# A hybrid GLA and MLA decoder layer: two token tiles run backwards, so that one 128-column matmul serves two tiles at each GLA level

## The chip, the cores and the metric

The kernel runs on one core of a Trainium2 chip. The metric is the device time of one launch in microseconds, of which three runs of the kernel before are shown. A profile of a further execution gives the trace. PE is the matrix engine, PEld its weight loads, DVE the vector engine, ACT the scalar engine, POOL the GpSimd engine, and SP issues most DMAs.

## The reference

One decoder layer on x of 512 tokens by 1024 columns, all in float32. A layer norm is followed by one projection w_in that yields q, k, v, r and a gate of rank 16 for gated linear attention (GLA, four heads, 128 key and 256 value columns each), latents for multi-head latent attention (MLA, eight heads) and two sets of branch gates. Then come the two attentions, their output projections, the gated merge, an output projection, a layer norm, and a squared-ReLU MLP of width 4096 with another layer norm. The part that the change touches is the GLA:

```python
log_a = jax.nn.log_sigmoid((a_lr @ w_gla_a2 + b_gla_a2).astype(jnp.float32)) / GLA_TAU
...
b = jnp.cumsum(gi, axis=2)
diff = b[:, :, :, None, :] - b[:, :, None, :, :]
decay = jnp.exp(jnp.where(causal[:, :, None], diff, -jnp.inf))
scores = jnp.einsum('bhid,bhjd,bhijd->bhij', qi, ki, decay)
o = jnp.einsum('bhij,bhjv->bhiv', scores, vi) + jnp.einsum('bhid,bhdv->bhiv', qi * jnp.exp(b), state)
state = jnp.exp(b_last)[:, :, 0, :, None] * state + jnp.einsum('bhjd,bhjv->bhdv', ki * jnp.exp(b_last - b), vi)
```

Taken over all chunks, the score of query i and key j (j not after i) is the sum over the key columns of q·k times the exponential of the log decays between j and i.

## The kernel before, in words

The 512 tokens are four tiles of 128 (`NT = 4`). Most products are made of float32 values split into two parts: `hi`, a rounded copy, and `lo`, the remainder (`split`, lines 106 to 115, and `pump`, lines 191 and 192, for weights). A product of two split operands is three matmuls: hi·hi, hi·lo and lo·hi (lines 247 to 249 with the activations moving and 281 to 283 with the weights moving). Weights come as a stream of entries: SP loads a raw tile `wraw` ahead of use, ACT rounds it to `whi` (L191), DVE forms the remainder `wlo` (L192), and PE uses both. Every engine works through its own instructions in the order in which the program was written, so an instruction that waits holds up all that stand behind it on that engine.

The program is written by Python generators. `spawn` puts one among the active ones, and each step of a large product calls `tick`, which advances the active ones by one `yield`. So the side work (norms, gates, GLA levels, attention) is laced between the matmuls of the large products, and the places of the `yield`s set the order.

The pieces that matter here:

- `prep` (L504 to L535) turns positions into the sine and cosine tables, and casts the level mask from the loaded int32 `lmi` to `lmask` (bytes) on DVE.
- `latents` (L594 to L630) makes the GLA log decays: the part `at` (L605) and the rounded `aT` (L606) on DVE, four matmuls into `z` (L611), `g` (L615) on DVE, the exponential and logarithm on ACT, and the final subtraction on POOL (L629).
- `r_prep` and `r_acc` (L695) load the weights of the r projection in combinations: SP loads one quarter (L700), and POOL then issues DMAs that add another onto it in place. There are eight such accumulating DMAs at the start, all in POOL's own software queue.
- `h_early` (L1091 to L1097) forms sums and differences of the normalised activations on DVE for the fast product of r.
- `gla_levels(h)` does the scores of one head by halving. At level s (1, 2, 4, ... 256) each block of 2s tokens has a left half of keys and a right half of queries, and the decay from a key to a query splits at the middle into two factors, neither of which exceeds one. `rp[:, 0]` holds the log decay from a token to the end of its block, `rp[:, 1]` that from the beginning of the block. `vec` takes the two exponentials on ACT (L800), multiplies them with k and q on DVE into `M` (L802, one instruction of 512 columns), and `advance` doubles the block on POOL (L794 and L795).
- For levels 2 to 64, line 856 multiplies, tile by tile, the columns of `M` up to the last key (128, 96 or 64 of them) with the 64 query columns of the tile: four matmuls a level. Level 128 (L860) is two matmuls of 128 by 128 and level 256 (L864) two of 128 by 256. These products are in plain float32, and each shows up as two matmul records. `take` copies the wanted entries of the result into `SD` under the mask `lmask` (L812).
- `proj_v` and `silu` evict v and r by head, 256 columns at a time (L112 from `proj_v`, L687).
- `gla_out` multiplies the scores with v, tile by tile.

```python
for tt in range(NT):
    c = slice(tt * P, (tt + 1) * P)
    mm(p[:rows(s), tt * 64:(tt + 1) * 64].rearrange("p (n s) -> p n s", s=s),
       M[:, tt * P:tt * P + rows(s)], pairs(M[:, c], s)[:, :, 1, :], start=True, stop=True)
```

Of the kernel before, what the change touches and what calls it, by code (L numbers as in the profile page):

```python
# [10 lines left out]
F32 = mybir.dt.float32  # L11
# [41 lines left out]
def tile_hybrid_block(ctx: ExitStack, tc: tile.TileContext, I, out, dbg=None):  # L53
# [41 lines left out]

    act = nc.scalar.activation
# [32 lines left out]
    ident = ca[:, 0:P]  # L129
    g_in = ca[:, P:P + NK]  # L130
# [3 lines left out]
    identr = consts.tile([P, P], F32R, name="identr")  # L134
    masks = consts.tile([P, T], F32, name="masks")
# [312 lines left out]
    def ln_transpose(rows, g, b, outs, hf, alt=False, n="h0"):  # L448
        tk = slice(hf * 256, (hf + 1) * 256)
        for k in range(NK):  # L450
# [3 lines left out]
            for i in range(2):  # L454
                nc.tensor.transpose(p[:, i * P:(i + 1) * P], rows[2 * hf + i][:, k * P:(k + 1) * P], ident)
# [27 lines left out]
    act(identr, ident, AF.Copy)  # L483
    cb = consts.tile([P, PACK_B - P], F32, name="cb")
    n0 = PACK_B - P - 32
    for dst, c0, n in ((cb[:, :n0], 0, n0), (masks[:, T - P:], n0, P), (cb[:, n0:], n0 + P, 32)):
        nc.scalar.dma_start(dst, I["c_pack_b"][:, c0:c0 + n])
# [9 lines left out]
    nc.gpsimd.memset(masks[:, :T - P], 0.0)  # L497
# [3 lines left out]
    cs2 = consts.tile([P, NT, ROPE], F32, name="cs2")  # L501
    sn2 = consts.tile([P, NT, ROPE], F32, name="sn2")

    def prep():  # L504
        with tc.issue_after(last_in.ins):
            vts(hbg, bgt, 0.5, None, op0=ALU.mult)
            nc.vector.tensor_copy(lmask, lmi)
        posf = consts.tile([P, NT], F32, name="posf")
        with tc.issue_after(last_in.ins):
            nc.vector.tensor_copy(posf, posi)  # L510
        ang = B([P, NT, 32], F32, "ang")
# [17 lines left out]
        act(sn2[:, :, 32:], angs[0], AF.Sin)  # L529
        act(cs2[:, :, :32], angs[1], AF.Sin)  # L530
        nc.vector.tensor_copy(cs2[:, :, 32:], cs2[:, :, :32])
        vts(sn2[:, :, :32], sn2[:, :, 32:], -1.0, None, op0=ALU.mult)
        yield

    def rope(src, cs, sn, dst, tmp, tmp2):  # L535
        vtt(tmp, src, cs, op=ALU.mult)
        vtt(tmp2[..., 0:32], src[..., 32:64], sn[..., 0:32], op=ALU.mult)
        vtt(tmp2[..., 32:64], src[..., 0:32], sn[..., 32:64], op=ALU.mult)
        gtt(dst, tmp, tmp2, op=ALU.add)
# [92 lines left out]
    def latents2():  # L632
# [5 lines left out]
        for tt in range(NT):  # L638
            src = lat[tt][:, LKR:LKR + ROPE]
            vtt(kt1[:, tt], src, cs2[:, tt], op=ALU.mult)  # L640
            vtt(kt2[:, tt, 0:32], src[:, 32:64], sn2[:, tt, 0:32], op=ALU.mult)
            vtt(kt2[:, tt, 32:64], src[:, 0:32], sn2[:, tt, 32:64], op=ALU.mult)
        vtt(kr, kt1, kt2, op=ALU.add)
# [15 lines left out]
    def lr(t2, s):  # L659
        v = t2[:, 0, :]  # L660
        return bass.AP(tensor=v.tensor, offset=v.offset, ap=[v.ap[0], [2 * s, T // (2 * s)], [T + s, 2], [1, s]])

    def pairs(v, s):
        return v.rearrange("p (n two s) -> p n two s", two=2, s=s)

    Vh = [None] * GH
    Rg = [None] * GH
    ogT = [None] * NK

    def proj_v(hp, guard=None):  # L670
        hs = (2 * hp, 2 * hp + 1)

        def e(a, j, ps):
            for i, h in enumerate(hs):
                if Vh[h] is None:
                    Vh[h] = (A([P, NT, HV], F32R, "vh"), A([P, NT, HV], F32R, "vl"))
                split(ps[:, i * HV:(i + 1) * HV], Vh[h][0][:, a, :], Vh[h][1][:, a, :])
        gemm_tm([PL["v", hp]], hT, T, e, guard=guard, fine=3)

    def silu(j, a, ps):  # L680
        th = B([P, T], F32, "th")
        act(th, ps, AF.Tanh, scale=0.5)
        for i in range(2):
            h = 2 * j + i
            if Rg[h] is None:
                Rg[h] = A([P, NT, HV], F32, "rg")
            stt(Rg[h][:, a, :], th[:, i * HV:(i + 1) * HV], 1.0, ps[:, i * HV:(i + 1) * HV],  # L687
                op0=ALU.add, op1=ALU.mult)
            rgn[h] += 1
# [88 lines left out]
    def rows(s):  # L778
        return P - s if s >= 32 else P

    def gla_levels(h):
# [8 lines left out]

        def advance(s):
            Rv, Pv = pairs(rp[:, 0, :], s), pairs(rp[:, 1, :], s)
            n = T // (2 * s)
            gtt(Rv[:, :, 0, :], Rv[:, :, 0, :], Pv[:, :, 1, s - 1:s].to_broadcast([P, n, s]), op=ALU.add)  # L794
            gtt(Pv[:, :, 1, :], Pv[:, :, 1, :], Pv[:, :, 0, s - 1:s].to_broadcast([P, n, s]), op=ALU.add)  # L795

        def vec(s):
            E = B([P, T], F32, "E")
            for w in range(2):
                act(pairs(E, s)[:, :, w, :], pairs(rp[:, w, :], s)[:, :, w, :], AF.Exp, scale=1.0 / 16.0)  # L800
            M = B([P, T], F32, "M")
            vtt(pairs(M, s), pairs(E, s), lr(qk, s), op=ALU.mult)  # L802
# [4 lines left out]
        def take(s, p):  # L807
            nonlocal s128, s256
            if s <= 64:
                n, m = 64 // s, rows(s)  # L810
                mk = lmask[:m, LEVELS.index(s), :].rearrange("p (n s) -> p n s", s=s)
                nc.vector.copy_predicated(  # L812
                    SDf[:m].rearrange("p (t n two s) -> p t n two s", t=NT, two=2, s=s)[:, :, :, 1, :],
                    mk[:, None].to_broadcast([m, NT, n, s]),
                    p[:m, :256].rearrange("p (t n s) -> p t n s", t=NT, s=s))
# [9 lines left out]
        act(q1, pairs(rp[:, 1, :], 1)[:, :, 1, :], AF.Exp, scale=1.0 / 16.0)  # L825
        xs = [B([P, 2, 192], F32, "x1") for _ in range(2)]
        for i in range(2):
# [3 lines left out]
                qk[:, 1, t2].rearrange("p (t n two) -> p t n two", t=2, two=2)[:, :, :, 1], op=ALU.mult)  # L831
# [12 lines left out]
        for i, p in enumerate(px1):  # L844
# [3 lines left out]
            nc.vector.copy_predicated(d.rearrange("p t (n two) -> p t n two", two=2)[:, :, :, 1],  # L848
                                      lmask[:, 0, None, :].to_broadcast([P, 2, 64]), pt[:, :, P:])
        prev = None  # L850
        while s < T:
            p = PX()
            if s <= 64:
                for tt in range(NT):
                    c = slice(tt * P, (tt + 1) * P)
                    mm(p[:rows(s), tt * 64:(tt + 1) * 64].rearrange("p (n s) -> p n s", s=s),  # L856
                       M[:, tt * P:tt * P + rows(s)], pairs(M[:, c], s)[:, :, 1, :], start=True, stop=True)
            elif s == 128:
                for i in range(2):
                    mm(p[:, i * P:(i + 1) * P], M[:, 2 * i * P:(2 * i + 1) * P],  # L860
                       M[:, (2 * i + 1) * P:(2 * i + 2) * P], start=True, stop=True)
# [17 lines left out]
    def gla_out(h):  # L879
        while SS[h] is None or Vh[h] is None or rgn[h] < NT:  # L880
            yield
# [9 lines left out]
        vh, vl = Vh[h]  # L891
        ss = S([P, NT], F32, "gss")
        ps = []
        for i in range(NT):
# [3 lines left out]
            for j in range(i + 1):  # L898
                mm(o, blk(j, i, 0), vh[:, j, :], start=j == 0, stop=False)
                mm(o, blk(j, i, 0), vl[:, j, :], start=False, stop=False)  # L900
                mm(o, blk(j, i, 1), vh[:, j, :], start=False, stop=j == i)
# [10 lines left out]
        for i in range(NT):  # L912
            o = ps[i // 2][:, (i % 2) * HV:(i % 2 + 1) * HV]
            stt(og[i // 2][:, i % 2, :], o, rs[:, i:i + 1], Rg[h][:, i, :], op0=ALU.mult, op1=ALU.mult)
        yield
        for kk in range(2):
            k = 2 * h + kk
            p = PX()
            for tt in range(NT):
                nc.tensor.transpose(p[:, tt * P:(tt + 1) * P], og[tt // 2][:, tt % 2, kk * P:(kk + 1) * P], ident)  # L920
# [13 lines left out]
    def tables():  # L934
        tab = A([P, 2, T], F32, "tab")
        for i, (src, c0) in enumerate(((cs2, 0), (sn2, 32))):
# [749 lines left out]
```

## Time and profile before

| quantity | value |
|---|---|
| runs (us) | 878.78, 880.04, 885.48; median 880.04 |
| profiled execution | 882.47 us, of which the span is 880.7 |
| granted TensorE clock | 0.997 |
| busy: PE, PEld | 861.2 us, 752.9 us |
| busy: DVE, ACT, POOL | 643.2, 470.2, 198.3 us |
| DMA | 134.60 MB in 95504 packets, 153 GB/s on average |
| level matmuls (L856) | 192 records, from 104.7 to 209.7 us |

The span runs from the first to the last instruction of the profiled execution; the time of that execution is slightly longer than its span. A row of a timeline reads: start, length, engine, line, operation, output <- input, shapes, count, and in brackets the idle time before it with what ended it. Consecutive instructions overlap on an engine, so the starts tell more than the lengths.

### The profile page before, as it was taken

What the parts mean: (1) busy time and instruction counts of PE and PEld (TensorE: products, weight loads), DVE (VectorE), ACT (ScalarE), POOL (GpSimd) and SP (SyncE); (2) the same over time, 40 slices, a digit from 0 to 9 for tenths busy, and PEclk for the clock granted to TensorE, in tenths of its full rate; (3) what the DMA queues carried; (4) which work ended last, traced back from release to release, by engine and by line L of the source; (5) the groups of instructions that cost most, each with busy time, mean ns of one, the idle gap of its engine ahead of it and who ended that gap; (6) DMA issues with size and microseconds to landing.
All of it is one profiled execution on the core that took longest, in us unless ns stands there. A gap on an engine that the chain in (4) does not pass through costs nothing.

```text
span 880.7 us, 13019 instructions
## 1 busy us (share of the span) xinstructions
PE 861.2 (98%) x4804; PEld 752.9 (85%) x4804; DVE 643.2 (73%) x1054; ACT 470.2 (53%) x835; POOL 198.3 (23%) x226
## 2 busy tenths in 40 slices
PE   6999999999999999999999999999999999999996
PEld 5988888889999978888888889988888888888985
DVE  7859969978665646767866878986567546778865
ACT  5556766556465624435655324575366446656820
POOL 1224637854101030300000022005301520141000
PEclk9999999999999999999999999999999999999998
DMA  7995936796638454322136446008922990497312
GB/s 249 277 229 151 328 107 160 227 225 198 163 104 199 130 142 102 102 66 79 49 120 243 140 144 216 1 1 251 259 64 51 299 222 3 104 251 198 120 62 81
DMA packets 95504, 134.60 MB, mean 153 GB/s; under 512 B 12960, under 2 KB 58400, under 8 KB 95440
## 3 DMA queue, kind: packets, MB, share of 16 engines
q1 hardware_dynamic: 73840, 92.36, 33.0%
q0 software_dynamic: 19392, 37.76, 20.0%
q10 hardware_dynamic: 2208, 3.66, 1.2%
q8 instruction: 38, 0.62, 0.3%
q14 instruction: 26, 0.21, 0.1%
HBM read 110.15 MB, written 8.91 MB: 135 GB/s over the span
## 4 chain that ended last, share of the span: by engine, by line
PE 92%; DVE 3%; DMA 2%; ACT 1%; issue 0%; POOLq 0%; SPq 0%; DVEq 0%; POOL 0%; ACTq 0%
PE mm L247 11%; PE mm L248 11%; PE mm L249 11%; PE mm L283 5%; PE mm L281 5%; PE mm L282 5%; PE mm L1210 4%; PE mm L1209 4%; PE mm L1208 4%; PE px L856 2%; PE px L1495 2%; PE px L1494 2%; PE px L1496 2%; DMA res<-ev 2%; PE mm L755 2%; PE mm L754 2%
## 5 line engine op out<-in xcount | busy, mean ns | idle before, releaser
L192 DVE TENSOR_TENSOR wlo<-wraw,whi 128x1024 fp32r<-128x1024 f32 (+1 forms) x102 | 102.0, 1009 | 82.3 <-ACT whi L191 79.2
L191 ACT ACTIVATE whi<-wraw 128x1024 fp32r<-128x1024 f32 (+1 forms) x102 | 86.5, 860 | 86.0 <-PE mm L248 46.6
L248 PE MATMUL mm<-h,whi 128*128 128x512 f32 x224 | 87.2, 389 | 0.0
L247 PE MATMUL mm<-h,whi 128*128 128x512 f32 x224 | 87.1, 390 | 0.0
L249 PE MATMUL mm<-h,wlo 128*128 128x512 f32 x224 | 83.2, 390 | 0.0
L1513 POOL DMA_DIRECT2D res<-ev x42 | 37.4, 1027 | 182.5 <-ACT ev L1511 152.6
L192 DVE TENSOR_TENSOR wlo<-wq,whi 128x1024 fp32r<-128x1024 f32 x44 | 54.5, 1238 | 28.0 <-ACT whi L191 27.9
L191 ACT ACTIVATE whi<-wq 128x1024 fp32r<-128x1024 f32 x44 | 46.5, 1056 | 28.4 <-PE mm L1209 20.0
L1210 PE MATMUL mm<-sh,wlo 128*128 128x256 f32 x176 | 49.9, 283 | 0.0
L1209 PE MATMUL mm<-sh,whi 128*128 128x256 f32 x176 | 49.8, 283 | 0.0
L1208 PE MATMUL mm<-sh,whi 128*128 128x256 f32 x176 | 49.8, 283 | 0.0
L249 PEld LDWEIGHTS mm<-h,wlo 128*128 128x128 f32 x224 | 42.0, 188 | 9.1 <-DVE wlo L192 0.4
L247 PEld LDWEIGHTS mm<-h,whi 128*128 128x128 f32 x224 | 42.1, 188 | 8.7
L248 PEld LDWEIGHTS mm<-h,whi 128*128 128x128 f32 x224 | 42.1, 188 | 8.7
L191 ACT ACTIVATE xh<-wraw 128x1024 fp32r<-128x1024 f32 (+1 forms) x28 | 27.2, 985 | 28.6 <-PE mm L283 16.7
L439 POOL TENSOR_TENSOR mv<-mv,mhalf 128x1 f32<-128x1 f32 x4 | 4.7, 1179 | 157.9 <-DVE mv L438 157.9
L800 ACT ACTIVATE E<-rp 128x256 f32<-128x256 f32 x64 | 26.2, 420 | 24.4 <-POOL rp L795 15.9
L192 DVE TENSOR_TENSOR xl<-wraw,xh 128x1024 fp32r<-128x1024 f32 (+1 forms) x28 | 31.3, 1128 | 8.5 <-ACT xh L191 8.5
L1559 ACT ACTIVATE relu<-mm 128x512 f32<-128x512 f32 x24 | 14.1, 596 | 42.0 <-PE mm L249 42.0
L794 POOL TENSOR_TENSOR rp<-rp 128x256 f32<-128x256 f32 x32 | 30.9, 965 | 22.3 <-ACT E L800 13.5
L971 POOL DMA_DIRECT2D QS<-q x32 | 16.0, 508 | 85.2 <-DMA wraw<-in_w_o_gla_dram 48.5
L795 POOL TENSOR_TENSOR rp<-rp 128x256 f32<-128x256 f32 x32 | 33.4, 1043 | 6.1 <-ACT q L825 2.7
(478 smaller groups left out, 2812.7 us busy)
## 6 DMA issues: line engine op xcount, KB each, us to landing
wraw<-in_w_ff_dram SPq DMA_DIRECT2D x36, 512.0 KB, 5.3
wraw<-in_w_in_dram SPq DMA_DIRECT2D x30, 512.0 KB, 5.1
wq<-in_w_ff_dram POOLq DMA_DIRECT2D x26, 512.0 KB, 9.3
res<-ev POOLq DMA_DIRECT2D x42, 256.0 KB, 9.1
wq<-in_w_in_dram SPq DMA_DIRECT2D x20, 512.0 KB, 6.7
wq<-in_w_in_dram POOLq DMA_DIRECT2D x18, 512.0 KB, 9.8
hsd<-hs SPq DMA_DIRECT2D x16, 256.0 KB, 4.8
xr<-hsd SPq DMA_DIRECT2D x16, 256.0 KB, 3.6
```

The source lines that it names most:

```text
L191: st["ins"] = act(hi[:, k, :n], raw[:, k, :n], AF.Copy)
L192: st["lo"] = vtt(lo[:, k, :n], raw[:, k, :n], f(hi[:, k, :n]), op=ALU.subtract)
L247: mm(o, hi[:, c], xh, start=first, stop=False)
L248: mm(o, hi[:, c], xl, start=False, stop=False)
L249: mm(o, lo[:, c], xh, start=False, stop=last)
L281: mm(o, xh, hi[:, :n], start=opens, stop=False, skip_group_check=share)
L282: mm(o, xh, lo[:, :n], start=False, stop=False, skip_group_check=share)
L283: mm(o, xl, hi[:, :n], start=False, stop=last, skip_group_check=share)
L1208: mm(oa, hi[:, k, c], xh, start=opens and k == 0 and a == 0, stop=False, skip_group_check=True)
L1209: mm(oa, hi[:, k, c], xl, start=False, stop=False, skip_group_check=True)
L1210: mm(oa, lo[:, k, c], xh, start=False, stop=k == 3, skip_group_check=True)
L1513: nc.gpsimd.dma_start(res[tt + t][:, j * T:(j + 1) * T], e, accum_op=ALU.add)
```

## The change

- The tokens of tiles 2 and 3 are stored in reverse order within their tile. That is done where the normalised input is transposed: the transposing matmul takes the identity with its columns reversed (`identJ`). What depends on token order follows: the positions of these tiles are turned by two small transposes, the causal mask of MLA gets a transposed version for them, the outputs are turned back by `identJ` in the transposes of `og` and of the attention weights, and the branch gates are written backwards.
- With that, in tiles 2 and 3 the queries of a block stand left and the keys right. At each level, `M` is laid out in two halves: 256 columns of keys and 256 of queries. The 64 keys of tile t and the 64 of tile t + 2 fill 128 columns, interleaved by blocks, as do their queries, so one matmul of 128 by 128 serves two tiles; two matmuls a level take the place of four. The columns of queries stand in two runs of 64.
- `M` is written by two DVE instructions of 256 columns instead of one of 512, each after its own exponential.
- The level mask now has 512 columns in the new order. The half for tiles 0 and 1 comes from the old load, the half for tiles 2 and 3 from seven further DMAs that POOL issues into a second, zeroed `lmi`, each shifted by s rows. Fourteen DVE casts take the place of one.
- The tables of sine and cosine are kept once, at 32 columns; `kr` is made by a subtraction and an addition.
- v and r of heads 2 and 3 are evicted by 512 columns at once into tiles that the two heads share.

In the order of instructions, the matmul engine has 48 level matmuls where there were 96 for levels 2 to 64, and three transposes more. DVE has 1095 instructions where there were 1056, ACT 791 for 796, POOL 240 for 231. On POOL the mask loads stand behind the fifth accumulating `wq` load and ahead of the sixth. On DVE, seven of the casts stand early (after the input's norms) and seven in the neighbourhood of `aT`: `at`, the first new cast, `aT`, the other six, and then the split of the next weight tile. SP issues 241 instructions as before; a few loads of `wraw` and `wq` change places by one.

```diff
+    def rev(ap):
+        dims = [list(d) for d in ap.ap]
+        step, n = dims[-1]
+        return bass.AP(tensor=ap.tensor, offset=ap.offset + step * (n - 1), ap=dims[:-1] + [[-step, n]])
+
+    def view(ap, off, *dims):
+        return bass.AP(tensor=ap.tensor, offset=ap.offset + off, ap=[list(ap.ap[0])] + [list(d) for d in dims if d[1] > 1])
...
+    identJ = rev(ident)
...
-                nc.tensor.transpose(p[:, i * P:(i + 1) * P], rows[2 * hf + i][:, k * P:(k + 1) * P], ident)
+                nc.tensor.transpose(p[:, i * P:(i + 1) * P], rows[2 * hf + i][:, k * P:(k + 1) * P],
+                                    identJ if hf and n == "h0" else ident)
...
-    act(identr, ident, AF.Copy)
...
-    lmask = consts.tile([P, len(LEVELS), 64], U8, name="lmask")
-    lmi = B([P, len(LEVELS), 64], I32, "lmi")
-    nc.scalar.dma_start(lmi, I["c_lmask"])
+    lmask = consts.tile([P, 512], U8, name="lmask")
+    lmi = [B([P, len(LEVELS), 64], I32, "lmi")]
+    nc.scalar.dma_start(lmi[0], I["c_lmask"])
+
+    def lm_load():
+        lmi.append(B([P, len(LEVELS), 64], I32, "lmi"))
+        nc.gpsimd.memset(lmi[1], 0)
+        for li, s in enumerate(LEVELS):
+            nc.gpsimd.dma_start(lmi[1][s:, li], I["c_lmask"][:P - s, li])
...
-            nc.vector.tensor_copy(lmask, lmi)
...
+        p = PX()
+        nc.tensor.transpose(p[:2, :P], posf[:, 2:], identJ)
+        nc.tensor.transpose(p[:, P:2 * P], masks[:, P:2 * P], ident)
...
+        nc.tensor.transpose(p[:, :2], pr, ident[:2, :2])
...
+        lm_load()
+        yield
+        act(sn, angs[0], AF.Sin)
+        act(cs, angs[1], AF.Sin)
+        yield
+        for s in LEVELS:
+            for d in range(2):
+                src = lmi[d][:, LEVELS.index(s), ::s]
+                nc.vector.tensor_copy(lm(s)[:, d], src[:, None].to_broadcast([P, 2, 64 // s]))
+        yield
...
+            if hp == 1:
+                if a % 2 == 0:
+                    t = [A([P, 2, T], F32R, n) for n in ("vh", "vl")]
+                    for h in hs:
+                        Vh[h] += [[x[:, i, h % 2 * HV:(h % 2 + 1) * HV] for x in t] for i in range(2)]
+                    Vt[hp] = t
+                split(ps, Vt[hp][0][:, a % 2], Vt[hp][1][:, a % 2])
+                return
...
+            stt(Vt["r", j, a // 2][:, a % 2], th, 1.0, ps, op0=ALU.add, op1=ALU.mult)
...
         def vec(s):
             E = B([P, T], F32, "E")
-            for w in range(2):
-                act(pairs(E, s)[:, :, w, :], pairs(rp[:, w, :], s)[:, :, w, :], AF.Exp, scale=1.0 / 16.0)
             M = B([P, T], F32, "M")
-            vtt(pairs(M, s), pairs(E, s), lr(qk, s), op=ALU.mult)
+            for w, src in enumerate((R, G)):
...
+                act(e, halves(src, s, w), AF.Exp, scale=1.0 / 16.0)
+                vtt(m, e, halves(qk[:, w, :], s, w), op=ALU.mult)
...
-                nc.vector.copy_predicated(
-                    SDf[:m].rearrange("p (t n two s) -> p t n two s", t=NT, two=2, s=s)[:, :, :, 1, :],
-                    mk[:, None].to_broadcast([m, NT, n, s]),
-                    p[:m, :256].rearrange("p (t n s) -> p t n s", t=NT, s=s))
+                n = P // s
+                mk = lm(s).rearrange("p d t n -> p d (t n)")
+                nc.vector.copy_predicated(halves(SDf, s, 1), mk[:, :, :, None].to_broadcast([P, 2, n, s]),
+                                          p[:, :256].rearrange("p (d n i) -> p d n i", d=2, i=s))
...
             if s <= 64:
-                for tt in range(NT):
-                    c = slice(tt * P, (tt + 1) * P)
-                    mm(p[:rows(s), tt * 64:(tt + 1) * 64].rearrange("p (n s) -> p n s", s=s),
-                       M[:, tt * P:tt * P + rows(s)], pairs(M[:, c], s)[:, :, 1, :], start=True, stop=True)
+                for t in range(2):
+                    mm(view(p, 64 * t, (P, 2), (1, 64)), M[:, t * P:(t + 1) * P],
+                       view(M, 256 + 64 * t, (P, 2), (1, 64)), start=True, stop=True)
...
-        act(gt[m][:, br, tk], ps, AF.Tanh, scale=0.5, bias=hbg[:, br * NK + m:br * NK + m + 1])
+        g = gt[m][:, br, tk]
+        if tk.start:
+            g, ps = rev(g.rearrange("p (t i) -> p t i", t=2)), ps.rearrange("p (t i) -> p t i", t=2)
+        act(g, ps, AF.Tanh, scale=0.5, bias=hbg[:, br * NK + m:br * NK + m + 1])
```

More of the change, by code (lines that the diff above doesn't have):

```diff
@@ L656, in latents2, with halves, last @@
         KKs.append(KK)
[L659 to L667, printed above, removed]
+    def halves(v, s, right, off=0):
+        if s >= P:
+            return view(v, off + s * right, (256, T // (2 * s)), (1, s))
+        return view(v, off + s * right, (256 - s if right else 256 + s, 2), (2 * s, P // s), (1, s))
+    def last(v, s, right):
+        if s >= P:
+            return view(v, 2 * s - 1 if right else s - 1, (129, T // (2 * s))).to_broadcast([P, T // (2 * s), s])
+        o = view(v, 2 * s - 1 if right else s - 1, (257 - 2 * s if right else 257, 2), (2 * s, P // s))
+        return o[:, :, :, None].to_broadcast([P, 2, P // s, s])
+    Vh = [[] for _ in range(GH)]
+    Rg = [[None] * NT for _ in range(GH)]
+    Vt = {}
     ogT = [None] * NK
@@ L824, in gla_levels @@
         q1 = B([P, NT, 64], F32, "q1")
-        act(q1, pairs(rp[:, 1, :], 1)[:, :, 1, :], AF.Exp, scale=1.0 / 16.0)
+        act(q1.rearrange("p (d t) n -> p d (t n)", d=2), halves(G, 1, 1), AF.Exp, scale=1.0 / 16.0)
         xs = [B([P, 2, 192], F32, "x1") for _ in range(2)]
@@ L830, in gla_levels @@
             vtt(xs[i][:, :, P:], q1[:, 2 * i:2 * i + 2, :],
[L831 removed]
+                qk[:, 1, t2].rearrange("p (t n two) -> p t n two", t=2, two=2)[:, :, :, 1 - i], op=ALU.mult)
         advance(1)
```

117 lines of the change are left out of this document (66 added, 51 removed).

## The prediction, as it was put on record

> **What bounds the kernel now.** I read the page first (its span, busy shares, chain), then busy time by stretch, then the timelines of PE, POOL and DVE around the edited places.
>
> ```profile
> span 880.7 us, 13019 instructions
> PE 861.2 (98%) x4804; PEld 752.9 (85%) x4804; DVE 643.2 (73%) x1054; ACT 470.2 (53%) x835; POOL 198.3 (23%) x226
> PE 92%; DVE 3%; DMA 2%; ACT 1%; issue 0%; POOLq 0%; SPq 0%; DVEq 0%; POOL 0%; ACTq 0%
> ...
> 0.00:22.00 22.00, 13.40 (x72) 12.11 (x73) 16.70 (x38) 12.73 (x21) 2.98 (x9) 1.00 0.78 249
> ...
> 66.00:88.00 22.00, 22.00 (x104) 18.04 (x103) 20.99 (x41) 14.30 (x28) 9.27 (x7) 1.00 0.53 151
> ...
> 132.00:154.00 22.00, 22.00 (x125) 18.55 (x124) 20.94 (x31) 14.87 (x30) 16.84 (x17) 1.00 0.66 161
> 154.00:176.00 22.00, 22.00 (x128) 18.67 (x127) 20.60 (x33) 13.29 (x26) 19.11 (x18) 1.00 0.70 226
> 176.00:198.00 22.00, 22.00 (x116) 18.74 (x115) 17.14 (x26) 11.20 (x28) 13.03 (x12) 1.00 1.00 227
> ```
>
> In the stretch rows the columns are: bounds, length, then busy time (count) of PE, PEld, DVE, ACT, POOL, then the granted clock, DMA share and GB/s. TensorE sets the end: 92% of the chain, 98% of the span, and full in every stretch shown after the first. So a microsecond taken from PE is worth a microsecond, unless something then keeps PE waiting. The reader should see two places where that can happen. In 132 to 176 us VectorE has only 1.06 and 1.40 us free in 22, and POOL 2.9 free in the second. In 66 to 88 us VectorE has 1.01 us free.
>
> **The gain: fewer matmuls in the GLA levels.** Lines L856 (levels 2 to 64) and L860 (level 128) on PE's timeline (start, length, engine, line):
>
> ```profile
> L856 PE MATMUL px<-M x192: 217/273/275, 104.7 to 209.7; 128*128 128x64 f32 x128, 128*96 128x64 f32 x32, 128*64 128x64 f32 x32
> 105.80 1.00 PE L856 MATMUL px<-M 128*128 128x64 f32 x8
> 106.61 0.47 PE L283 MATMUL mm<-whi,h 128*128 128x512 f32 x1
> 106.92 0.39 PE L281 MATMUL mm<-whi,h 128*128 128x512 f32 x1
> ...
> 113.50 0.81 PE L856 MATMUL px<-M 128*96 128x64 f32 x8
> 114.13 0.48 PE L281 MATMUL mm<-whi,h 128*128 128x512 f32 x1
> ...
> 116.39 0.68 PE L856 MATMUL px<-M 128*64 128x64 f32 x8
> 116.99 0.50 PE L281 MATMUL mm<-whi,h 128*128 128x512 f32 x1
> ...
> 119.19 0.61 PE L860 MATMUL px<-M 128*128 128x128 f32 x4
> 119.55 0.47 PE L281 MATMUL mm<-whi,h 128*128 128x512 f32 x1
> 119.86 0.39 PE L282 MATMUL mm<-wlo,h 128*128 128x512 f32 x1
> ```
>
> Matmuls overlap, so I price each group by the start of what comes next. A level takes four matmuls (eight records, two for each fp32 product): 106.61 − 105.80 = 0.81 us with 128 rows, 114.13 − 113.50 = 0.63 with 96, 116.99 − 116.39 = 0.60 with 64. After the change every such level is two matmuls of 128 rows and 128 columns. That is exactly the form L860 already has: 119.55 − 119.19 = 0.36 us. The matmul behind each group is delayed alike (0.31 us to its successor, at 106.61 and at 119.55), so that cancels. L860's columns lie in one run and the new ones in two of 64; 0.81 − 0.36 halves records of 0.10 and 0.09 us each, so I take the number of records as what counts.
>
> A head has four levels of the first kind, one of the second, one of the third: 4 × 0.45 + 0.27 + 0.24 = 2.31 us. The 192 records are 24 groups of eight, four heads of six: 4 × 2.31 = **9.2 us off PE**. If the two-run columns were slow, up to the price of the old 64-column record twice, nothing would be saved: bound 0 to 9.2.
>
> The Trainium skill, "TensorE: Matmul & The Clock Gate", section "LDWEIGHTS (loading the stationary operand)", prices a weight load by its columns alone, about 107 ns for 128; by it, four loads fewer save an estimated 0.43 us on a 128-row level, against the 0.45 above. It would also make 96 and 64 rows dearer when they become 128, which the 0.63 and 0.60 already hold.
>
> **What it adds on PE.** Three small transposes (positions forth and back, the triangular mask) at about 35 and 40 us: priced by the last rows' 0.09 to 0.12 us a record, five to six records' worth with their wait, 0.35 us (0.2 to 0.6).
>
> **What it moves: the second half of the level mask.** Now `lmask` is one VectorE cast early on. After the change there are 14 casts. Seven read the old load and stand early (about 1 us of VectorE at 21 to 24 us, where the first row leaves it 5 us free; I take 0.2 us, 0 to 0.5). Seven read seven new POOL DMAs of 256 B rows, one per level, zeroed first by a POOL memset. These stand in POOL's queue behind the fifth of eight accumulating `wq` loads (L695); the sixth and seventh of them wait, by their reused semaphores, for the third and fourth of those to land; the last three accumulates come after them.
>
> ```profile
> 40.94 1.20 POOL L695 DMA_DIRECT2D wq<-in_w_in_dram  x1 [1.70 <-DMA wq<-in_w_in_dram]
> 43.79 1.20 POOL L695 DMA_DIRECT2D wq<-in_w_in_dram  x1 [1.65 <-DMA wq<-in_w_in_dram]
> ...
> wq<-in_w_in_dram POOLq DMA_DIRECT2D x1, 512.0 KB, 11.4
> wq<-in_w_in_dram POOLq DMA_DIRECT2D x1, 512.0 KB, 12.5
> QS<-q POOLq DMA_DIRECT2D x32, 64.0 KB, 1.9
> wraw<-in_w_in_dram SPq DMA_DIRECT2D x30, 512.0 KB, 5.1
> ...
> q0 software_dynamic: 810, 1.58, 61.4%
> q1 hardware_dynamic: 1204, 2.34, 46.4%
> ```
>
> The two 512 KB rows (size, us to landing) belong to the issues at 40.94 and 43.79: landed at 52.3 and 56.3. The third row is the quickest kind of POOL DMA elsewhere in the trace. The queue rows are for 36 to 50 us (packets, MB, share of 16 engines): the DMA engines are full. The new loads are issued at about 45 to 50 and, for the last, 52.3 us. If the software queue keeps order, they land just behind the fifth accumulate, about 55 to 58 us; the three later accumulates, issued later than now, leave room, and their target is used only after 120 us. If they overtake, the last lands 1.9 us after its issue at 52.3, about 54.2. SP issues the same loads, a few `wraw` and `wq` one place apart; they are asked for well ahead, so nothing (one late is 5.1 us by the `wraw` row). ACT loses one copy and writes 16 gate rows backwards, long after 264 us beside a full PE: nothing.
>
> Who waits? On VectorE they stand in this order: `at` (L605), first new cast, `aT` (L606), the other six casts, then the `wlo` split.
>
> ```profile
> 50.23 0.42 DVE L606 CAST aT<-at 16x512 fp32r<-16x512 f32 x1
> 54.11 1.23 DVE L192 TENSOR_TENSOR wlo<-wraw,whi 128x1024 fp32r<-128x1024 f32 x1 [3.46 <-ACT whi L191]
> 56.01 1.41 DVE L615 TENSOR_SCALAR g<-px,cb 128x512 f32<-128x512 f32 x2 [0.67 <-ACT az L613]
> ...
> 67.68 2.31 DVE L192 TENSOR_TENSOR wlo<-wraw,whi 128x1024 fp32r<-128x1024 f32 x1
> 54.85 0.63 PE L611 MATMUL px<-aT,wa 80*128 80x512 f32 x2
> 70.05 0.50 PE L249 MATMUL mm<-h,wlo 128*128 128x512 f32 x1
> ```
>
> `aT` feeds the PE matmul at 54.85, so today it has some 4 us of slack; PE itself will come there 0.55 us later (transposes, early casts). With a landing at 56.3, the cast (0.25, less columns than `aT`'s 0.42) and `aT` end at 57.0 and PE, due at 55.4, waits about 1.6 us. The other casts then end near 58, so `wlo` starts 3.9 us later than its 54.11. From 56.01 VectorE is contiguous up to the `wlo` that ends at 69.99 and is used at 70.05: no slack there at all. PE, already 0.55 + 1.6 late, waits the remainder: 3.9 − 2.15 ≈ 1.7. Sum 3.3 us; I take **3.0 us** (0 with a landing by 54.5; 1.5 to 5 for 55 to 58, one for one beyond).
>
> The Trainium skill, "DMA: Bandwidth & Descriptors", section "Why a DMA increments its semaphore by 16 and not by 1", speaks against this change: the number of engines of a DMA must divide its outermost count, so that 127 rows go through one engine, though it adds that software-queue copies have been seen on all 16. No run here shows which; the third rival below prices it from rows.
>
> **What it adds on VectorE, ACT and POOL in the levels.** The product `M` (L802) becomes two halves; v and r of heads 2 and 3 are evicted 512 wide.
>
> ```profile
> 114.35 0.45 DVE L812 COPY_PREDICATED SD<-lmask,px 96x256 f32<-96x256 uint8 x1 [0.61 <-PE px L856]
> ...
> 122.33 0.75 DVE L112 TENSOR_TENSOR vl<-mm,vh 128x256 fp32r<-128x256 f32 x2 [0.27 <-ACT vh L111]
> ...
> 140.01 0.68 DVE L728 TENSOR_TENSOR er<-mm,er 128x512 f32<-128x512 f32 x1
> 140.61 0.68 DVE L802 TENSOR_TENSOR M<-E,qk 128x512 f32<-128x512 f32 x1
> ...
> 143.39 0.42 DVE L812 COPY_PREDICATED SD<-lmask,px 128x256 f32<-128x256 uint8 x1
> ...
> 145.47 0.76 DVE L802 TENSOR_TENSOR M<-E,qk 128x512 f32<-128x512 f32 x1 [0.61 <-ACT E L800]
> ...
> L795 POOL TENSOR_TENSOR rp<-rp 128x256 f32<-128x256 f32 x32 | 33.4, 1043 | 6.1 <-ACT q L825 2.7 <-ACT E L800 1.4
> ```
>
> 512 columns step on after 0.60 us (140.01 to 140.61); two 256-wide ones take 0.75 less their 0.08 of overlap, 0.67. So a split `M` costs 0.07: 8 × 0.07 = 0.56 us a head. The four `vl` pairs and four `rg` pairs joined give 8 × 0.07 = 0.56 back, once. Predicates grow from 96 or 64 rows to 128; the two rows give 0.45 with 96 and 0.42 with 128: nothing. POOL's L794/L795 keep their sizes: nothing, covered as before by the neighbouring levels; without cover each costs its 1.04 us.
>
> In 127 to 176 us, where VectorE was already full, PE cannot run 2.3 us a head ahead of it. Head 1 asks PE to arrive 2.3 us sooner, VectorE has 1.06 us free and 0.56 more to do, so its part is up to 2.3 − 0.5 = 1.8 us, given back partly by 176 to 198 us (4.9 free). I take **1.3 us** lost (0 to 3).
>
> **Sum.** −9.2 + 0.35 + 0.2 + 3.0 + 1.3 = −4.35 us. The profiled execution took 882.47 us (span 880.7 and 1.8 around it): 878.1. The three runs' median, 880.04, is 2.4 below that execution: **875.7 us**. A run of this kernel tells about 1% (8.8 us) from no change.
>
> **The rivals.**
> *All of it arrives.* The mask loads land by 54.5 us and the levels' VectorE work is hidden: −9.2 + 0.55 = −8.65, so 871.4. For: DMA landings are not strictly ordered by issue. Against: VectorE's 1.06 us.
>
> *Gain eaten in the levels.* Each head's chain POOL, ACT, VectorE, PE decides, not PE: POOL is 19.11 of 22 busy, VectorE 20.60. Then the levels return about 2.3 + 2.3 + 1.5 us, instead of 1.3: −9.2 + 0.55 + 3.0 + 6.1 = +0.45, 880.5: nothing to see. For: the 0.61 waits for `E` at 145.47. Against: heads 0 and 3 lie where VectorE has air. The same 880 comes if the new matmul saves nothing and the rest is hidden, that is, the change does not do what it says.
>
> *Slower: the first mask load is late.* 127 rows on one engine: the queue rows give 0.464 × 16 × 14 / 1204 = 0.086 us a packet in the hardware queue, 0.614 × 16 × 14 / 810 = 0.17 in the software one; 127 × 0.086 = 11 us (to 22) behind the 56.3 landing, so 67. The `wlo` at 54.11 then starts near 68.9, 14.8 us late, less PE's own 0.55: −9.2 + 0.55 + 14.2 + 1.3 = +6.9, so 886.9 (898 at 0.17). From a landing at about 60.4 us on, the sum is above the old time. Against: packets of 256 B are an eighth of those.
>
> **How the numbers follow.** Chances: forecast 0.42, all arrives 0.30, eaten 0.15, late load 0.13. The forecast's own range, with its terms' bounds, is 872 to 880. The range to hold 8 in 10 takes in the first two rivals, 3 us below the first for terms I have not seen (shorter head chains, say), and the lower half of the third: 868 to 887. Faster by over 1% (below 871.2) needs the whole gain: some 0.6 of the first rival, and 0.06 for those unseen terms, 0.24. Slower by over 1% (above 888.8) needs a landing past 69 us, half of the third rival and a little of the second: 0.09. Within: 0.67.
>
> **What would show it.** In the profile after: the level matmuls as 96 records of 128 columns, groups 0.36 apart; a VectorE wait of the first new cast on a `lmi` DMA, ending at 55 to 58 us, with a PE wait for `aT` near 55; PE's wait for `wlo` near 72; few waits of PE on `M` in 130 to 176. Wrong if the cast waits past 62 or not at all, if the groups take over 0.5 us, or if PE idles over 3 us in the levels.

## The result and the profile after

| | before | after |
|---|---|---|
| median of 20 runs (us) | 880.97 | 879.00 |
| range (us) | 878.78 to 885.48 | 876.86 to 881.32 |
| profiled span (us) | 880.7 | 876.3 |

The ratio after to before is 0.9966, 95% interval 0.9952 to 0.9981: a gain of 3.0 us (1.7 to 4.2). It agrees with the quotient of the means (878.83 and 881.80) and not with that of the medians, which lie 2.0 us apart, because eight of the 20 runs before took 882.79 to 885.48 us and none of the 20 after took more than 881.32. Line numbers moved: `wlo` is L200 now, the level matmuls L912, `M` L862, POOL's additions in `advance` L846 and L847, `aT` L634, its matmul L639, the mask casts L566.

Busy time by stretch after (bounds, length, busy time and count of PE, PEld, DVE, ACT, POOL, then clock, DMA share, GB/s):

```profile
0.00:22.00 22.00, 12.72 (x66) 11.42 (x67) 15.60 (x35) 12.44 (x20) 2.35 (x9) 1.00 0.74 244
...
44.00:66.00 22.00, 21.10 (x102) 17.67 (x101) 13.31 (x36) 11.31 (x17) 8.76 (x11) 1.00 0.88 190
66.00:88.00 22.00, 20.44 (x96) 16.77 (x95) 20.92 (x42) 13.58 (x26) 8.66 (x6) 1.00 0.62 176
...
110.00:132.00 22.00, 21.77 (x110) 18.20 (x109) 18.45 (x36) 13.42 (x29) 7.25 (x10) 1.00 0.38 120
132.00:154.00 22.00, 20.45 (x106) 17.39 (x105) 22.00 (x36) 14.11 (x27) 14.01 (x15) 1.00 0.66 160
154.00:176.00 22.00, 21.49 (x106) 17.67 (x104) 20.86 (x34) 15.32 (x31) 17.76 (x19) 1.00 0.64 209
176.00:198.00 22.00, 20.45 (x110) 17.57 (x110) 17.66 (x35) 11.45 (x28) 11.95 (x13) 1.00 1.10 252
198.00:264.00 66.00, 65.98 (x518) 64.15 (x517) 50.07 (x77) 41.60 (x84) 18.46 (x18) 1.00 0.56 159
264.00:876.30 612.30, 604.21 (x3266) 524.13 (x3264) 431.46 (x688) 310.03 (x518) 89.32 (x117) 1.00 0.48 133
sum 876.30, PE 852.61 PEld 744.97 DVE 648.48 ACT 470.41 POOL 198.61; mean PE 77.51 PEld 67.72 DVE 58.95 ACT 42.76 POOL 18.06
```

The kernel before from 22 us on, by the same view:

```profile
22.00:264.00 242.00, 242.00 (x1464) 215.77 (x1463) 194.61 (x329) 146.76 (x296) 105.95 (x101) 1.00 0.70 197
...
264.00:880.70 616.70, 605.76 (x3272) 524.98 (x3271) 431.90 (x688) 310.69 (x519) 89.42 (x117) 1.00 0.47 132
```

PE was full from 22 to 264 us before; now it has gaps there. What it waited for (us in total, times, longest), after and then before:

```profile
PE px L463 <- ACT x L451: 9.1, 1, 9.1
PE mm L257 <- DVE wlo L200: 1.6, 1, 1.6
PE mm L810 <- DVE wraw L200: 1.6, 1, 1.6
PE mm L290 <- DVE wlo L200: 1.2, 1, 1.2
PE px L639 <- DVE aT L634: 0.9, 1, 0.9
PE px L912 <- DVE SD L872: 0.6, 2, 0.3
...
PE px L912 <- DVE M L862: 0.5, 1, 0.5
```

```profile
PE px L455 <- DMA wraw<-in_w_in_dram: 8.4, 1, 8.4
PE px L1210 <- DVE wlo L192: 2.0, 1, 2.0
```

The two spans differ by 4.4 us. PE's busy time and its gaps add up to that:

| part | us |
|---|---|
| PE busy, 861.2 to 852.6 | −8.6 |
| 0 to 22: the first matmul starts at 9.1 instead of 8.4 | +0.7 |
| 44 to 88: 0.90 + 1.56 idle, the mask's two waits | +2.5 |
| 110 to 198: 0.23 + 1.55 + 0.51 + 1.55 idle, the GLA levels | +3.8 |
| from 264 on: 8.1 idle against 10.9 | −2.8 |

The first and the last gap are not work of the change's. The first matmul starts at 8.5 us in a second profile of the changed kernel, and at 8.3, 8.4 and 10.0 in three other profiles below. The 2.0 us wait at L1210 of the kernel before stands in the profiles of the run with halves of M and of the run with doubled levels too, and is missing in others, with code there that is the same. Without these two parts the change's own terms are −8.6 + 2.5 + 3.8 = −2.3 us. So the profiles' 4.4 flatters the change; the runs' 3.0 counts. Whether the change makes that late wait rarer, which would be part of the 3.0, no run here shows.

Of the 3.8 us in the levels, 2.8 are waits for the weight parts `wraw` and `wlo` that VectorE makes, and 1.1 are waits for `SD` and `M`. So what PE lacks there is VectorE's work in general, not `M` alone.

The mask's waits, on VectorE's timeline after:

```profile
50.84 0.68 DVE L633 TENSOR_TENSOR at<-px,aT 16x512 f32<-16x512 f32 x1 [2.55 <-ACT aT L631]
56.65 0.23 DVE L566 CAST lmask<-lmi 128x128 uint8<-128x128 int32 x1 [5.12 <-DMA lmi<-in_c_lmask_dram]
56.91 0.42 DVE L634 CAST aT<-at 16x512 fp32r<-16x512 f32 x1
57.35 0.60 DVE L566 CAST lmask<-lmi 128x64 uint8<-128x64 int32 x6
57.86 1.22 DVE L200 TENSOR_TENSOR wlo<-wraw,whi 128x1024 fp32r<-128x1024 f32 x1
...
71.72 2.31 DVE L200 TENSOR_TENSOR wlo<-wraw,whi 128x1024 fp32r<-128x1024 f32 x1
```

And on PE's:

```profile
57.47 0.70 PE L639 MATMUL px<-aT,wa 80*128 80x512 f32 x2 [0.90 <-DVE aT L634]
...
74.08 0.50 PE L257 MATMUL mm<-h,wlo 128*128 128x512 f32 x1 [1.56 <-DVE wlo L200]
...
108.71 0.61 PE L912 MATMUL px<-M 128*128 128x128 f32 x4
109.07 0.48 PE L290 MATMUL mm<-wlo,h 128*128 128x512 f32 x1
```

The first cast waited 5.12 us for its load and held `aT` and a weight split behind it; PE paid 0.90 and 1.56 of that. A level's matmuls take 109.07 − 108.71 = 0.36 us, as forecast.

### The profile page after: what moved, and what is told of

Its sections match the earlier page's. It is cut to its first block, busy times and chain, and to the rows that moved or that the text cites. A ratio compares the mean times of both kernels' runs of the same rounds, so it can differ in the third digit from the quotient of the medians.

```text
span 876.3 us, 12888 instructions
## 1 busy us (share of the span) xinstructions
PE 852.6 (97%) x4711; PEld 745.0 (85%) x4711; DVE 648.5 (74%) x1093; ACT 470.4 (54%) x830; POOL 198.6 (23%) x235
## 4 chain that ended last, share of the span: by engine, by line
PE 86%; DVE 8%; DMA 3%; issue 1%; ACT 1%; POOL 0%; POOLq 0%; SPq 0%; DVEq 0%; ACTq 0%
PE mm L255 10%; PE mm L256 10%; PE mm L257 10%; PE mm L291 5%; PE mm L290 4%; PE mm L289 4%; PE mm L1268 4%; PE mm L1266 4%; PE mm L1267 4%; PE px L1556 2%; PE px L1557 2%; PE px L1555 2%; DVE M L862 2%; PE mm L1556 2%; PE mm L1557 2%; PE mm L1555 2%
## 5 line engine op out<-in xcount | busy, mean ns | idle before, releaser
L200 DVE TENSOR_TENSOR wlo<-wraw,whi 128x1024 fp32r<-128x1024 f32 (+1 forms) x102 | 100.5, 994 | 78.1 <-ACT whi L199 73.9
L200 DVE TENSOR_TENSOR wlo<-wq,whi 128x1024 fp32r<-128x1024 f32 x44 | 55.1, 1252 | 28.1 <-ACT whi L199 28.1
L862 DVE TENSOR_TENSOR M<-E,qk 128x256 f32<-128x256 f32 x64 | 37.6, 616 | 0.2 <-ACT E L861 0.2
L200 DVE TENSOR_TENSOR xl<-wraw,xh 128x1024 fp32r<-128x1024 f32 (+1 forms) x28 | 31.3, 1127 | 8.8 <-ACT xh L199 8.8
L846 POOL TENSOR_TENSOR rp<-rp 128x256 f32<-128x256 f32 x32 | 30.3, 946 | 24.8 <-ACT E L861 15.1
```

Source lines behind the costliest of these rows:

```text
L200: st["lo"] = vtt(lo[:, k, :n], raw[:, k, :n], f(hi[:, k, :n]), op=ALU.subtract)
L862: vtt(m, e, halves(qk[:, w, :], s, w), op=ALU.mult)
```

## The experiments

All ratios are to the kernel before. The theory after the result: the matmuls gave about what was counted, the mask loads took 2.5 back, and the levels took 3.8 back because VectorE, delayed by POOL's additions, could not feed PE earlier. Rivals: the matmuls gave less; the split of `M` alone is the loss; the chain through POOL is.

**Mask loads at the start.**

```diff
     nc.gpsimd.memset(masks[:, 2 * P:5 * P], 0.0)
+    lm_load()
...
-        lm_load()
-        yield
```

> The changed kernel, with the seven mask loads (and the memset ahead of them) issued by POOL at the start, where it idles from 9.9 to 22.3 us, in place of behind the fifth accumulate. If the wait of the casts is what held PE at aT (0.9 us) and at the wlo (1.6 us), both waits go and the kernel is 2.5 us below the changed one: 876.5, a ratio of 0.995 to the kernel before. Rival: VectorE, full from 132 to 176 us, would have taken the time anyway; then the time stays near 879 and PE's waits in the levels grow by as much.

Measured 0.9948 (0.993 to 0.9966), median 877.19. Both waits are gone; those in the levels are the same, and so are the gaps there, 3.73 us in the last row:

```profile
PE px L463 <- DMA posi<-in_positions_dram: 8.3, 1, 8.3
PE mm L809 <- DVE wraw L200: 1.6, 1, 1.6
PE mm L290 <- DVE wlo L200: 1.2, 1, 1.2
...
110.00:198.00 88.00, 84.27 (x427) 70.97 (x426) 78.88 (x138) 54.30 (x113) 51.39 (x55) 1.00 0.70 185
```

So the waits were real cost, and PE's gaps in the levels did not grow, where the rival had them grow by as much. Run again on one chip beside the changed kernel:

> The changed kernel once more, beside the early-mask kernel on the same chip, so that the two can be set against each other: 0.9966 of the kernel before, as measured (0.995 to 0.998).

> The early-mask kernel once more, on the same chip as the changed kernel: if the 2.5 us of the mask's two waits are real gain, 0.994 to 0.995 of the kernel before and 1.6 to 2.5 us below the changed kernel. Rival: no difference between the two beyond 1 us.

Measured 0.9960 (0.9945 to 0.9974; median 878.08) for the changed kernel and 0.9948 (0.993 to 0.9966; 876.09) with early masks. Both times the early loads are 1.1 to 2 us better, by the ratios and by the medians. That is less than the trace's 2.5, and the intervals overlap, so whether all of the 2.5 arrives is open.

**Each level matmul twice.** It puts PE's work back and leaves VectorE's alone.

```diff
-                for t in range(2):
+                for t in (0, 1, 0, 1):
```

> The changed kernel, with each new level matmul issued twice (the second writes the same result over the first). This puts PE work back: groups of 8 records take 0.81 us in the changed kernel's trace, groups of 4 take 0.36, so 24 x 0.45 = 10.8 us. If PE sets the end throughout the levels: +10.8 us over the changed kernel (889.8, ratio 1.009). If PE's idle time there (3.8 us from 110 to 198) takes up part: +7 (886, 1.006). If POOL, ACT and VectorE set the pace of the levels: 0 to +3 (880.5, 1.000).

Measured 1.0081 (1.0052 to 1.011), 10 us above the changed kernel. The profile is of the slowest of its seven runs (893.34 us, median 887.49), so only the stretch of the levels is read from it. There PE is idle for 1.81 us, where it was 3.84:

```profile
110.00:198.00 88.00, 86.19 (x467) 73.71 (x466) 74.62 (x130) 52.12 (x109) 48.32 (x51) 1.00 0.61 165
```

So of 10.8 us, 2.0 went into gaps. The interval (some 3 us either way) does not tell 8.8 from 10.8, but the third reading is out: PE's work sets the pace for most of the levels, and the gain was real. This refutes the prediction's rival by which the gain is eaten in the levels.

**Halves of M in the kernel before.**

```diff
-            vtt(pairs(M, s), pairs(E, s), lr(qk, s), op=ALU.mult)
+            for w in range(2):
+                vtt(pairs(M, s)[:, :, w, :], pairs(E, s)[:, :, w, :], lr(qk, s)[:, :, w, :], op=ALU.mult)
```

> The kernel before, with each M product written by two VectorE instructions of 256 columns in place of one of 512, and nothing else. If the split costs 0.07 us a pair, as the prediction priced it, 0.56 a head: 0 to +1 us (ratio 1.000 to 1.001). Rival: beside POOL each half pays for the contention in full (the changed kernel's mean of a half is 616 ns, half of the old one 454, so 0.3 us a pair), and where VectorE is full that reaches PE: +2.5 to +3.5 us (1.003 to 1.004).

Measured 1.0068 (1.0042 to 1.0093), +6.0 us (3.7 to 8.2): more than either. The groups before and with halves, and the stretch of the levels with halves:

```profile
L802 DVE TENSOR_TENSOR M<-E,qk 128x512 f32<-128x512 f32 x32 | 28.8, 901 | 3.5 <-ACT E L800 3.4
```

```profile
L803 DVE TENSOR_TENSOR M<-E,qk 128x256 f32<-128x256 f32 x64 | 37.8, 618 | 0.2 <-ACT E L800 0.2
...
110.00:198.00 88.00, 85.47 (x464) 71.80 (x463) 74.21 (x134) 52.43 (x108) 48.17 (x52) 1.00 0.66 174
```

A pair costs 2 × 618 against 901 ns, 0.34 us more, and PE, full before, now has 2.5 us of gaps in the levels. Where the other 3.5 of the runs' 6.0 come from is not shown. The profile is 5.5 us longer than that of the kernel before, and of these 1.5 are a first matmul that starts later (10.0), 0.5 are gaps after 264 us and 0.8 a busier PE. The runs themselves spread widely, from 882.74 to 892.86 us.

**No additions on POOL, in the changed kernel and in the one before.**

```diff
-            if s < 256:
-                advance(s)
             return M
```

> The changed kernel without POOL's additions of the log decays at levels 2 to 128 (those at level 1 stay), so the scores are not the right ones; only the times of the VectorE instructions count. If VectorE's halves of M are slow because POOL's additions run beside them, their mean falls from 616 ns to about 420 with the same access patterns and PE's idle time of 3.8 us from 110 to 198 us goes. Rival: the patterns themselves are slow (two runs, broadcast pieces): the mean stays near 600.

> The kernel before, without POOL's additions at levels 2 to 128 (its scores are not the right ones; only time counts). In the kernel before PE has no idle time from 22 to 264 us, so taking POOL's contention away should bring nothing: 0 to -0.5 us (ratio 0.9995 to 1.000), although M's mean falls from 0.90 to about 0.68 us. That would show that the changed kernel's loss is the old contention, met by a PE that asks sooner. Rival: the additions slow the kernel before as much as the changed one (-5 us, 0.994): then they are no reason for the lost part of the gain.

The changed kernel without them: 873.49 us in its one run, some 5 us below the changed kernel. The kernel before without them: 1.0000 (0.9975 to 1.0024). The groups of `M` and the stretch of the levels, changed kernel without additions, then the changed kernel itself, then the kernel before without additions:

```profile
L862 DVE TENSOR_TENSOR M<-E,qk 128x256 f32<-128x256 f32 x64 | 24.3, 423 | 2.3 <-ACT E L861 2.2
...
110.00:198.00 88.00, 88.00 (x453) 75.58 (x453) 70.47 (x143) 55.46 (x117) 19.05 (x18) 1.00 0.70 186
```

```profile
L862 DVE TENSOR_TENSOR M<-E,qk 128x256 f32<-128x256 f32 x64 | 37.6, 616 | 0.2 <-ACT E L861 0.2
```

```profile
L802 DVE TENSOR_TENSOR M<-E,qk 128x512 f32<-128x512 f32 x32 | 21.5, 688 | 0.9 <-ACT E L800 0.8
...
110.00:198.00 88.00, 88.00 (x489) 75.38 (x487) 66.74 (x116) 54.13 (x115) 19.83 (x18) 1.00 0.69 182
```

This settles the levels. With the same access patterns a half takes 423 ns without the additions and 616 with them, and without them all of PE's 3.8 us of gaps go. The kernel before gains nothing from the same cut: the delays were there, hidden behind a busier PE. The exponentials `E` wait for the additions too, but that chain is not the reason: the halves of `M` waited for `E` for 0.2 us in all (the row of the changed kernel), and ahead of the gaps at 148.1 and 174.5 to 178.8 us VectorE worked without a pause from 127.7 and 160.0 us on. One pair of rows shows how it works (after, VectorE and then POOL):

```profile
142.77 1.26 DVE L862 TENSOR_TENSOR M<-E,qk 128x256 f32<-128x256 f32 x1
143.95 0.68 DVE L783 TENSOR_TENSOR er<-mm,er 128x512 f32<-128x512 f32 x1
144.55 0.41 DVE L862 TENSOR_TENSOR M<-E,qk 128x256 f32<-128x256 f32 x1
```

```profile
142.65 1.08 POOL L846 TENSOR_TENSOR rp<-rp 128x256 f32<-128x256 f32 x1
143.81 0.70 POOL L847 TENSOR_TENSOR rp<-rp 128x256 f32<-128x256 f32 x1
144.59 0.85 POOL L846 TENSOR_TENSOR rp<-rp 128x256 f32<-128x256 f32 x1
```

The first half of `M` begins with POOL's addition under way and ends 0.3 us behind it, at 144.03; `er`, which reads one operand from a matmul bank, keeps its 0.68 beside an addition; the second half, which begins ahead of its addition, takes 0.41. The whole trace says the same. Of the 64 halves, 34 begin with an addition under way, and 33 of these end 0.28 to 0.37 us behind that addition's end, however much of it was left; they take 0.79 us on average, the other 30 take 0.41. In the kernel before, 24 of the 32 whole products begin during an addition and end 0.55 to 0.66 us behind it; the other 8 take 0.68 to 0.71. So a product of two on-chip operands waits for the addition under way, whatever its own length, and two short ones can be caught twice. The Trainium skill, "GPSIMD Engine Reference", section "1. Specifications", says that POOL shares its interfaces to the on-chip memory with VectorE and that they contend where VectorE has two such inputs; these rows agree.

The additions thus delay `M` by 64 × (616 − 423) ns = 12.35 us in the changed kernel, and by 32 × (901 − 688) ns = 6.82 us in the kernel before. From the first to the last `M`, VectorE's 181 instructions take 120.0 us in the changed kernel and 102.9 without the additions; of these 17.1 us, 12.3 are the products', 2.7 the weight parts', and the rest falls on other instructions of two on-chip operands. `er` takes 677 ns with them and 674 without.

**M in one instruction, on the kernel with early masks.** Once with the halves of tiles 2 and 3 exchanged in storage, once for its time alone.

```diff
-                vtt(m, e, halves(qk[:, w, :], s, w), op=ALU.mult)
...
+            M = A([P, 768], F32, "M") if 1 < s < P else B([P, T], F32, "M")
...
+                vtt(view(M, 256, (2 * s, T // (2 * s)), (s - 256, 2), (1, s)), pairs(E, s), lr(qk, s), op=ALU.mult)
```

> The kernel with early mask loads (0.9948 of the kernel before), with M made by one VectorE instruction of 512 columns again for levels 2 to 64 and 256: the rows of q and k, and of the two log decays, are stored with the parts of tiles 2 and 3 exchanged, so that one access pattern meets keys and queries of all four tiles, and M has 768 columns, of which the middle 256 are the packed keys. The matmuls stay 128 by 128. If the two halves of M cost the levels their 2.5 to 4 us of PE idle: 873.5 to 874.5 (ratio 0.992). Rival: POOL's additions set the pace of the levels, whatever VectorE does: 877 (0.995).

```diff
-                vtt(m, e, halves(qk[:, w, :], s, w), op=ALU.mult)
+            vtt(M, E, qk[:, 0, :], op=ALU.mult)
```

> The kernel with early mask loads, with M in one plain VectorE product of 512 contiguous columns behind both exponentials; half of the columns then meet the wrong operand (q and k are not told apart), so only its time counts. The same two theories as for the run with exchanged storage: 873.5 to 874.5 (0.992) if the halves of M are the cost, 877 (0.995) if not. If this one is faster and the other is not, the strided writes or the 768-column tile cost what the single instruction saves.

The exchanged storage gave 1.0054 (1.0032 to 1.0077), far from both. In 198 to 220 us alone PE is idle for 5.6 us, and the granted TensorE clock there (the column behind POOL's) is 0.90, against 1.00 in the early-mask kernel:

```profile
198.00:220.00 22.00, 16.36 (x84) 13.68 (x83) 14.62 (x21) 10.51 (x20) 15.18 (x13) 0.90 0.76 185
```

The 768-column tile is taken from another pool of tiles (`A` for `B`); that this holds up other tiles was not tried apart, so the run tells nothing of the question. The plain version gave 0.9938 (0.9915 to 0.996) against 0.9948, too close to tell. Its profile has 2.6 us of PE gaps in the levels, against 3.7 with halves:

```profile
110.00:198.00 88.00, 85.42 (x434) 72.28 (x433) 74.11 (x117) 56.44 (x118) 60.11 (x59) 1.00 0.70 186
```

By these two profiles the split is about 1 us of the loss. That the rest is the delay which one product of 512 columns and the weight parts still meet beside POOL fits the run without additions, where all gaps go; it was not tried apart.

**The additions on VectorE, on the kernel with early masks.**

```diff
-            gtt(halves(R, s, 0), halves(R, s, 0), last(G, s, 1), op=ALU.add)
+            vtt(halves(R, s, 0), halves(R, s, 0), last(G, s, 1), op=ALU.add)
...
```

> The kernel with early mask loads, with the additions of the log decays on VectorE in place of POOL. VectorE gets 64 instructions of some 0.34 us (21.8 us over four heads), and loses the contention: M's halves fall from 616 to about 420 ns (12.5 us over 64), the weight splits beside them from 1.6 to 1.22. If VectorE's total sets the levels: +2 to +5 us over the early-mask kernel (879 to 882, 0.997 to 1.001), with VectorE full in 132 to 176. Rival: the shorter chain without POOL's 0.7 to 1.5 us an addition is what PE waits for: -2 us (875, 0.9925).

Measured 0.9991 (0.9973 to 1.0009), 3.8 us above its base, within the first theory's range. `M` falls to 416 ns, but PE's gaps in the levels grow to 4.7 us, and in 198 to 220 us PE is idle for 2.3 more at a granted clock of 0.92:

```profile
L861 DVE TENSOR_TENSOR M<-E,qk 128x256 f32<-128x256 f32 x64 | 26.5, 416 | 2.6 <-ACT E L860 2.6
...
110.00:198.00 88.00, 83.27 (x424) 70.65 (x423) 80.93 (x181) 55.14 (x115) 14.11 (x13) 1.00 0.62 168
...
198.00:220.00 22.00, 19.71 (x120) 17.60 (x120) 19.87 (x41) 12.56 (x25) 0.00 (x0) 0.92 0.66 171
```

So of the loss in the profile only 1.0 us stands in the levels. Another 2.2 are gaps right behind them, at the end of which the granted clock is half for 3.4 us (from 212.6 us on). The run still speaks against POOL's chain: the chain is gone, and PE waits longer for VectorE's work.

**Evictions: 256 wide again for heads 2 and 3; 512 wide for v of heads 0 and 1 too.**

```diff
-            if hp == 1:
+            if False:
...
-        if j == 1:
+        if False:
...
```

> The changed kernel, with v and r of heads 2 and 3 evicted by head, 256 columns at a time, as before. By the prediction's price, 8 x 0.07 = 0.56 us of VectorE more, of which part reaches PE: 0 to +0.6 us over the changed kernel (ratio to the kernel before 0.9966 to 0.9973). Rival: the joined evictions release matmul banks later or earlier and matter more than their length: beyond 1.5 us either way.

```diff
-            if hp == 1:
+            if True:
```

> The kernel with early mask loads, with v of heads 0 and 1 evicted 512 wide too. VectorE saves 4 x 0.07 us between 120 and 132 us, where it has some 3.5 us free: 0 to -0.5 us (ratio 0.9945 to 0.995). Rival: as with heads 2 and 3, where going back to 256 columns put a PE wait of 1.6 us on an eviction, the form decides a wait: -1.5 us (0.993).

Going back to 256: 0.9988 (0.9972 to 1.0004), 1.9 us above the changed kernel's 0.9966, though the intervals overlap, with a wait that the changed kernel does not have:

```profile
PE mm L1266 <- DVE vl L120: 1.6, 1, 1.6
```

The wait is as the rival had it; by the intervals the size is not sure. Going on to 512 for v of heads 0 and 1: 0.9975 (0.9957 to 0.9994) against 0.9948 (0.993 to 0.9966), slower by 2.4 us, where nothing or a gain was expected, again with intervals that overlap. Its profile has more PE waits for `M` than the early-mask kernel, which has 0.5 us of them, and 5.4 us of gaps in the levels in place of 3.7:

```profile
PE px L911 <- DVE M L861: 2.9, 5, 1.7
```

In these two profiles the form of an eviction moves waits by a microsecond or two, in either direction; why the second one loses was not followed up.

## Why the prediction was right or wrong, point by point

- **The sum: right in direction and range, too large by about half.** −4.35 forecast; a gain of 3.0 us measured (1.7 to 4.2), within 1% as thought likeliest. 875.7 was 3.3 below the median, of which 0.9 is the median of before, taken from three runs. The change's own terms in the profile are −2.3 us; the levels alone took 2.5 more than forecast. That the profiled −4.4 agrees is luck: the tail gave 2.8 by a wait that no term of the change accounts for.
- **The gain in PE, −9.2: right.** 96 records, 0.36 us a group. PE's busy time fell by 8.6, with three transposes more (forecast −9.2 + 0.35); putting the matmuls back cost 10 us.
- **The mask, +3.0: right in place, order and size.** The cast was released at 56.65 (55 to 58 forecast), the `wlo` behind it started at 57.86 (58.0), PE waited 0.90 for `aT` (1.6) and 1.56 for `wlo` (1.7): 2.5 in all. The early loads took both waits away.
- **Rival of the late load: refuted.** On POOL's empty queue the load of 127 rows landed in 2.3 us; in the changed kernel it took 11.4, as the accumulate just ahead of it (11.9). The seven loads landed in the order of issue, from 56.55 to 57.61, right behind the accumulate at 56.38. Order in the queue was the cause, not one slow engine: at that rival's price, one engine would have taken 11 us on the empty queue too. The 2.3 us agree with the exception that the Trainium skill adds to its rule of one engine ("DMA: Bandwidth & Descriptors", section "Why a DMA increments its semaphore by 16 and not by 1"); which engines took part, the trace does not tell. The row with early loads, then the two after:

```profile
lmi<-in_c_lmask_dram POOLq DMA_DIRECT2D x1, 31.8 KB, 2.3
```

```profile
wq<-in_w_in_dram POOLq DMA_DIRECT2D x1, 512.0 KB, 11.9
lmi<-in_c_lmask_dram POOLq DMA_DIRECT2D x1, 31.8 KB, 11.4
```

- **The levels, +1.3: the term that was mis-sized.** 3.8 us of PE gaps. The place was right (VectorE, full in 132 to 154); the price was not. "So a split `M` costs 0.07" came from a pair of evictions that read a matmul bank, which POOL does not delay. Without the additions it holds: 2 × 423 − 688 = 158 ns by lengths, less the 0.08 us of overlap, is 0.08. Beside POOL the same sum gives 2 × 618 − 901 = 335 ns, less the overlap 0.26. And the gaps reach from 132 to 198 us, over two heads, not one. The 3.8 lies beyond the stated bounds of 0 to 3 and short of the rival's 6.1; by the prediction's own sign (PE idle over 3 us in the levels) it was wrong on this point.
- **The evictions, −0.56 of VectorE: probably mis-sized.** They seem to be worth 1.9 us, by one wait of 1.6, though the intervals overlap. If so, this and the levels' loss partly cancel, which is luck.
- **Rival that all arrives: what is left of it.** With early masks the kernel stands at 0.9948 twice, the best here of the versions that compute the layer; without POOL's additions one run gave 873.5 with the mask's wait still in it.

## What to carry to other kernels

An instruction's price comes from a row with the same kinds of operands and the same neighbours: an eviction from a matmul bank says nothing of a product of two on-chip tiles beside POOL. Before taking work off a full engine, look at which engine would have to arrive earlier in that stretch, and count its contention, which was hidden so far. A small load that is needed soon does not belong behind large ones in the same queue, and a cast that waits for it does not belong ahead of what the full engine needs.

## What the hardware showed unexpectedly

A short VectorE product that begins during a POOL addition ends 0.28 us or a little more behind it, and so can take three times its length (1.26 us, 0.41 alone); a product split in two can pay the neighbour twice. That taking all of this delay away gives nothing in the kernel before (1.0000) and some 5 us in the one run of the changed one was not expected in that sharpness.
